# Phase tables of a state-space branch: from doubling on VectorE to sine and double angle on GpSimd and ScalarE

## The chip, the cores and the metric

The kernel runs on one core of a Trainium2 chip. The metric is the device time of one execution in microseconds (us), from the first to the last instruction and what lies around it. The engines are TensorE (PE in the rows, with its weight loads as PEld), VectorE (DVE), ScalarE (ACT), GpSimd (POOL) and SyncE (SP), which issues nearly all transfers. Each engine takes its instructions strictly in the order in which the program issued them.

## The reference, cut to what matters

One step of a decoder layer: 2048 prompt positions and 8 sample positions of width 1024. One input projection feeds a causal convolution branch (31 taps, layer norm, SiLU gate) and a state-space (SSM) branch; both are gated, merged, projected and normalised. The SSM branch, with 32 groups of 64 complex states:

```python
dt = exp(log_dt); mag = exp(a_re * dt)
lb = mag * (cos(a_im * dt) + i sin(a_im * dt))        # one step of a state
bb = ((lb - 1) / a) * b
s[t] = lb * s[t-1] + bb @ u[t];  y[t] = Re(c @ s[t]) + d * u[t]
```

The kernel computes the recurrence in blocks of 8 positions. A block multiplies a state by lb to the 8th power, that is by rho = mag to the 8th and a turn by 8 times the angle. The turn is taken out: the inputs of the block recurrence are turned back by k times that angle (k = 0 to 127), a real scan with factor rho runs, and its results are turned forward again. The cosines and sines of k times the angle, for 16 x 128 states and 128 values of k, are the phase tables.

## The kernel before, in words

The prompt is done in two halves of 1024 positions (`half`, from line 1078), the sample positions with the first. Weights come as 512 KB tiles by SP (`w_dma`), two buffers; ACT casts a tile's high part (`whi`, line 251) and POOL subtracts it for the low part (`wlo`, through `ew`, line 331). `stages` (lines 276 to 296) does three matmuls for each product, high by high, high by low and low by high (lines 288 to 290), into one of six PSUM banks, which ACT or DVE evicts. A first half's stage of one weight tile lasts some 11 us. The order of the stages is: embedding, `sx` (SSM inputs, eight short stages), then for eight column tiles the gate `sg` (a sigmoid on ACT) and `u` (a product on DVE), then further gates.

All other work is written as generators (tasks) that `Background` interleaves with the stages at the time the program is built. A task yields an engine and a ready time; `use` adds a fixed charge to that engine's clock (`cV`, `cS`, `cG` for DVE, ACT and POOL, such as 0.08 + n / 960 us); `pump` always takes the task that can start first by these clocks, up to the matmul clock. So the charges fix, in advance, where in each engine's order an instruction lies. On the chip only semaphores count: if an instruction comes later than charged, whatever is queued behind it on its engine, and on others that need it, waits.

The task `ssm_setup` (lines 448 to 658, priority 6) first computes dt, mag and the angle on DVE (32 and 7 small instructions; L180, L183 and L177 are the helpers `ts`, `stt` and `tt`, tile `spar`), a sine and half-angle sine on ACT (L481, L482), the powers of lb and the product `bb`; POOL copies the reversed powers and fills the block tables `cbd` (L522 to L537). It then makes the phase tables (tile `ph`) on DVE, in two halves of 8 state columns: three doublings bring the angle to 8 times its value, then seven doublings along k fill 128 values. Each doubling normalises a complex number and does a complex product of six instructions:

```python
while m < P:
    unit_length(un[0][:, :, m - 1], un[1][:, :, m - 1], s2)
    cmul(un[0][:, :, m:2 * m], un[1][:, :, m:2 * m], un[0][:, :, 0:m], un[1][:, :, 0:m], *base, ...)
    m *= 2
    r0 = use("V", 2.0 + 6 * cV(4 * m), r0)
```

Behind them, in four rounds, come the product tables: DVE computes `gt` from `pwr` and `bb` (six instructions of 128x512, tile `gw`), PE transposes it (L609) and multiplies it with `cbd` (L619), ACT and DVE copy the results (`we`, L612; `kd`), POOL computes `cq` (six instructions, L645), and SP writes everything to DRAM (`we_d`, `tt_d`, `cq_d`, `ph_d`).

`ssm_batch` (four per half) waits in the planner for its round's tables, reads `we` and the phases, multiplies on PE (L719), turns and scans on DVE, and ends in more matmuls (L774, L777). `conv_task` does the convolution taps on DVE into PSUM (`acc`, L183) and, if eight of the 38 shared buffers (`units`) are free, hands part of them to `conv_side`, which lets ACT scale (`cq`, L881) and POOL add (`ca`, L331). `rms_task` sums squares (`re`, `rt`, L984) for later norms. The embedding's and the first norm's splits (`hh`, `hl`) feed the `sx` stages.

Of the kernel before, what the change touches and what calls it, by code (L numbers as in the profile page):

```python
# [13 lines left out]
P = 128  # L14
# [119 lines left out]
def build(nc, tc, A, O):  # L134
# [23 lines left out]
    with ExitStack() as ctx:  # L158
# [53 lines left out]
        P_OF = {k: 8 // v for k, v in KT_OF.items()}  # L212
        BLOCKS = [[(0, 344), (344, 344), (688, 344)], [(0, 512), (512, 512)]]
        PARTS = [[[0], [1, 2]], [[0], [1]]]
        TOK = [HT + NS, HT]

        order = []
# [210 lines left out]
            tt(oim, t1, t2, ALU.add)  # L428

        MAGIC = 12582912.0  # L430

        def exp_dve(out, x, w, ki):

# [10 lines left out]
            ts(ki, k, 127.0, 8388608.0, ALU.add, ALU.mult)  # L444
            tt(out, q, ki.bitcast(F32))

        tables = {"done": 0}

        def ssm_setup():
            yield from room(4)  # L450
# [16 lines left out]
            exp_dve(dt, k3, (k1, k2), ki)  # L467
            tt(th, are, dt)
            exp_dve(mag, th, (k1, k2), ki)
            r0 = use("V", 5.6, 3.0)  # L470
            yield "V", r0
            tt(th, aim, dt)
            ts(k1, th, 0.15915494309189535, MAGIC)
# [2 lines left out]
            stt(th, k1, -1.9350051879882812e-3, th, ALU.mult, ALU.add)  # L476
            stt(th, k1, -3.0199157663446332e-7, th, ALU.mult, ALU.add)
            ts(th, th, -3.1415925, 3.1415925, ALU.max, ALU.min)
            r0 = use("V", 1.6, r0)
            yield "S", r0  # L480
            S.activation(out=sn, in_=th, func=AF.Sin)  # L481
            S.activation(out=k1, in_=th, func=AF.Sin, scale=0.5)  # L482
# [19 lines left out]
            tt(k2, nre, aim)  # L502
            tt(k1, k1, k2, ALU.subtract)
            tt(fim, k1, k3)
            r0 = use("V", 4.0, r0)
            yield "V", r0

            def powers(t, top):
# [13 lines left out]
                    GP.tensor_copy(out=pwrev[r][:, p, :], in_=pw[r][:, 7 - p, :])  # L522
            fb = [f.rearrange("p (j x) -> p j x", x=1).to_broadcast([P, NJ, 16]) for f in (fre, fim)]
            cmul(b3(bb, 0), b3(bb, 1), fb[0], fb[1], b3(bcu, 0), b3(bcu, 1), b3(bb, 2), b3(bb, 3))
            r0 = use("V", 6.0, r0)
            use("G", 1.5, r0)
            GP.memset(zero, 0.0)
            yield from room(2)
# [10 lines left out]
            yield None, r1  # L539
            for b in range(NB):  # L540
                dma(out=tt_d[b], in_=zero.rearrange("p (q x) -> p q x", q=1).to_broadcast([P, 8, P]))

            yield "V", r0
            tt(k1, mag, mag)
            tt(k1, k1, k1)
            tt(rho, k1, k1)
            ph = [[k1, k2], [k3, nre]]

            def unit_length(re, im, t):

                tt(t[0], re, re)
                tt(t[1], im, im)
                tt(t[0], t[0], t[1], ALU.add)
                ts(t[0], t[0], -0.5, 1.5)
                tt(re, re, t[0])
                tt(im, im, t[0])

            v2 = [wk[:, x * 16:x * 16 + 16] for x in range(2)]
            V.tensor_copy(out=ph[0][0], in_=cs)
            V.tensor_copy(out=ph[0][1], in_=sn)  # L560
            for x in range(3):
                unit_length(*ph[0], v2)
                cmul(*ph[1], *ph[0], *ph[0], *v2)
                ph.reverse()
            r0 = use("V", 6.5, r0)
            for x in range(2):
                yield from room(3)
                pu2 = [alloc(name="ph") for _ in range(3)]
                un = [t[:, 0:1024].rearrange("p (j k) -> p j k", k=P) for t in pu2[0:2]]
                w2 = [pu2[2][:, y * 512:(y + 1) * 512].rearrange("p (j k) -> p j k", j=8) for y in range(2)]  # L570
                s2 = [t[:, 0:8] for t in v2]
                yield "V", r0
                for r in range(2):
                    V.tensor_copy(out=un[r][:, :, 0], in_=ph[0][r][:, x * 8:x * 8 + 8])
                m = 1
                while m < P:
                    unit_length(un[0][:, :, m - 1], un[1][:, :, m - 1], s2)
                    base = [u_[:, :, m - 1:m].to_broadcast([P, 8, m]) for u_ in un]
                    cmul(un[0][:, :, m:2 * m], un[1][:, :, m:2 * m], un[0][:, :, 0:m], un[1][:, :, 0:m],
                         *base, w2[0][:, :, 0:m], w2[1][:, :, 0:m])  # L580
                    m *= 2
                    r0 = use("V", 2.0 + 6 * cV(4 * m), r0)
                    yield "V", r0
                for b in range(2 * x, 2 * x + 2):
                    for r in range(2):
                        dma(out=ph_d[b][:, r * 512:(r + 1) * 512],
                            in_=pu2[r][:, (b - 2 * x) * 512:(b - 2 * x + 1) * 512], after=r0)
                free(*pu2)
            r1 = max(r0, r1)
            for b in range(NB):  # L590
                js = slice(b * 4, b * 4 + 4)
                yield from room(6)
                gt = alloc(name="gt")
                wt = alloc(name="gw")
                v4 = lambda t, r: t[:, r * 512:(r + 1) * 512].rearrange("p (j d c) -> p j d c", d=8, c=16)
                pr = [pwrev[r][:, :, js].rearrange("p d (j c) -> p j d c", c=1).to_broadcast([P, 4, 8, 16])
                      for r in range(2)]
                br = [b3(bb, r)[:, js, :].rearrange("p j (d c) -> p j d c", d=1).to_broadcast([P, 4, 8, 16])
                      for r in range(2)]
                yield "V", r1  # L600
                cmul(v4(gt, 0), v4(gt, 1), pr[0], pr[1], br[0], br[1], v4(wt, 0), v4(wt, 1))
                r1 = use("V", 6 * cV(512), r1)
                we = alloc(name="we")
                wev = we[:, 0:1024].rearrange("p (j i r s) -> p j i r s", i=2, r=2, s=64)
                for r in range(2):
                    yield "P", r1
                    pt = bank()
                    for j in range(4):
                        T.transpose(pt[:, j * P:(j + 1) * P], gt[:, r * 512 + j * P:r * 512 + (j + 1) * P], ident)  # L609
                    r2 = use("P", 0.5, r1)  # L610
                    yield "S", r2
                    S.copy(out=wev[:, :, :, r, :], in_=pt.rearrange("p (j i s) -> p j i s", i=2, s=64))  # L612
                    r2 = use("S", cS(512), r2)
                yield "P", r1
                pt = bank()
                for j in range(4):
                    o = pt[:, j * 32:(j + 1) * 32]
                    for r in range(2):
                        T.matmul(o, gt[:, r * 512 + j * P:r * 512 + (j + 1) * P],  # L619
                                 cb[r][:, b * 4 + j].rearrange("p i c -> p (i c)"), start=r == 0, stop=r == 1)  # L620
                r3 = use("P", 1.0, r1)
                free(gt)
                yield "V", r3
                kdu = alloc(name="kd")
                kd, dd = [kdu[:, x * 128:(x + 1) * 128].rearrange("p (c g) -> p c g", g=8) for x in range(2)]
                q3 = slice(96, 128)
                tt(dd[q3], dtile[q3, b * 8:b * 8 + 8].rearrange("p (c g) -> p c g", c=1).to_broadcast([32, 16, 8]),
                   ident[q3, 112:128].rearrange("p (c g) -> p c g", g=1).to_broadcast([32, 16, 8]))
                V.tensor_copy(out=kd, in_=pt[:, 0:128].rearrange("p (g c) -> p c g", c=16))
                tt(kd[q3], kd[q3], dd[q3], ALU.add)  # L630
                r3 = use("V", 0.8, r3)
                yield None, max(r2, r3)
                dma(out=we_d[b], in_=we[:, 0:1024])
                for q in range(8):
                    dma(out=tt_d[b][0:(q + 1) * 16, q, :],
                                 in_=kdu[(7 - q) * 16:128, 0:128])
                free(kdu, we)
                cq = alloc(name="cq")
                pr = [pw[r][:, 1:9, js].rearrange("p d (j c) -> p j d c", c=1).to_broadcast([P, 4, 8, 16])
                      for r in range(2)]  # L640
                cr = [c3[r][:, js, :].rearrange("p j (d c) -> p j d c", d=1).to_broadcast([P, 4, 8, 16])
                      for r in range(2)]
                yield "G", r1
                t1, t2 = v4(wt, 0), v4(wt, 1)
                g = lambda o, x, y, op=ALU.mult: GP.tensor_tensor(out=o, in0=x, in1=y, op=op)  # L645
                g(t1, pr[0], cr[0])
                g(t2, pr[1], cr[1])
                g(v4(cq, 0), t1, t2, ALU.add)
                g(t1, pr[0], cr[1])
                g(t2, pr[1], cr[0])  # L650
                g(v4(cq, 1), t1, t2, ALU.subtract)
                r2 = use("G", 6 * cG(512), r1)
                yield None, r2 + 2.0
                dma(out=cq_d[b], in_=cq[:, 0:1024])
                free(cq, wt)
                tables["done"] = b + 1
                tables[b] = queue["data"] + 1.0
            free(bb, bcu, cbd, pu)


# [14 lines left out]
        def ssm_batch(h, b, sx, ysb, n, ready):  # L675
# [22 lines left out]
            yield from room(4)  # L698
            we = alloc(name="swe")
            r = max(r, dma(out=we[:, 0:1024], in_=we_d[b], after=tables[b]))  # L700
            phu = alloc(name="sph")
            rp = dma(out=phu[:, 0:1024], in_=ph_d[b], after=tables[b])
            sc = alloc(name="sc")
            X = sc[:, 0:1096].rearrange("p (r j s) -> p r j s", r=2, j=4)
            yield "V", 0.0
# [20 lines left out]
                        S.copy(out=smp[:, rr, b * 4 + j0:b * 4 + j0 + 2, :], in_=pvs[rr][:, :, 128:136])  # L726
                    r1 = use("S", 0.56 if first else 0.36, r1)
            free(we)
            r = max(r1, rp)
            tmp, tm2 = alloc(name="stmp"), alloc(name="stmq")  # L730
            E = X[:, :, :, 9:137]
            t1 = tmp[:, 0:1024].rearrange("p (r j s) -> p r j s", r=2, j=4)
# [853 lines left out]
```

## Time and profile before

| | |
|---|---|
| median of three runs | 1972.55 us (1971.04 to 1973.43) |
| the profiled execution's own time | 1971.99 us |
| its span, first to last instruction | 1970.2 us |
| mean granted clock of TensorE | 0.989 of full speed |
| PE busy | 1918.5 us, 97% of the span |
| DVE busy | 1442.1 us, 73% |
| ACT busy | 765.6 us, 39% |
| POOL busy | 784.8 us, 40% |

The rows give, for a group of instructions, their line, engine and operation, the tiles written and read, the shape and count, the busy time and the mean of one; in a timeline the start and length in us, and in brackets how long the engine sat idle before and which instruction ended that. A granted clock of 1.00 is 2.4 GHz and 0.50 is 1.2 GHz. Matmul records overlap, since matmuls are pipelined; the chain of waits gives the step from one to the next.

### The profile page before, as it was taken

Reading aid. Unit: us, or ns where it says so; the run is one execution under the profiler, and the core shown is the slowest. Engines: PE = TensorE matmul, PEld = TensorE weight load, DVE = VectorE, ACT = ScalarE, POOL = GpSimd, SP = SyncE. Lnnn points to the kernel's source line nnn. Section 1 sums busy time; section 2 is a strip of 40 time slices with the busy share of each in tenths; the row PEclk is TensorE's granted clock in tenths of the full one; section 3 lists DMA queues with packets and bytes.
Section 4 is the critical chain, followed back from the end, with each engine's and each line's share of the span. In section 5 each row is a group of like instructions: output and inputs, shape, how many; then the busy total and the mean of one; then the engine's idle time right before and its main releaser. Section 6 shows DMA issues by size and latency. Waiting matters only on the chain.

```text
span 1970.2 us, 26641 instructions
## 1 busy us (share of the span) xinstructions
PE 1918.5 (97%) x10386; PEld 1723.0 (87%) x10386; DVE 1442.1 (73%) x1696; ACT 765.6 (39%) x1276; POOL 784.8 (40%) x573
## 2 busy tenths in 40 slices
PE   8897999999999999999899999999999999999998
PEld 7797999999999999999798788888888888888877
DVE  6889997899899876444884479888589843442686
ACT  7424211227311364254532223444731353223542
POOL 1437623315422223253533222687743222224554
PEclk9998999999999999999899999999999999999999
DMA  8461344542122215342554463212212211422455
GB/s 315 155 203 62 100 133 141 177 144 78 51 83 78 102 50 193 116 142 93 190 197 164 172 200 123 74 60 91 71 48 75 97 67 43 160 107 77 148 189 174
DMA packets 103286, 243.58 MB, mean 124 GB/s; under 512 B 11752, under 2 KB 44648, under 8 KB 103144
## 3 DMA queue, kind: packets, MB, share of 16 engines
q1 hardware_dynamic: 102840, 241.68, 36.2%
q8 instruction: 81, 1.33, 0.3%
q14 instruction: 45, 0.37, 0.1%
q10 hardware_dynamic: 320, 0.20, 0.0%
HBM read 188.17 MB, written 54.62 MB: 123 GB/s over the span
## 4 chain that ended last, share of the span: by engine, by line
PE 85%; issue 4%; DVE 4%; POOL 2%; ACT 1%; DMA 1%; POOLq 0%; ACTq 0%; SPq 0%; DVEq 0%
PE bank L288 27%; PE bank L290 26%; PE bank L289 26%; PE bank L774 2%; POOL wlo L331 1%; PE bank L777 1%; PE bank L719 1%; DMA raw<-in_w 1%; POOL ca L331 1%; DVE sgp L331 1%; DVE o L183 0%; DVE o L331 0%; DVE ml L331 0%; DVE spar L183 0%; PE bank L308 0%
## 5 line engine op out<-in xcount | busy, mean ns | idle before, releaser
L331 POOL TENSOR_TENSOR wlo<-raw,whi 128x512 fp32r<-128x512 f32 x386 | 566.5, 1486 | 1082.2 <-ACT whi L251 1064.5
L288 PE MATMUL bank<-hh,whi 128*128 128x344 f32 (+1 forms) x1888 | 665.9, 353 | 0.9 <-ACT whi L251 0.9
L289 PE MATMUL bank<-hl,whi 128*128 128x344 f32 (+1 forms) x1888 | 659.9, 350 | 6.8 <-DVE hl L331 6.8
L290 PE MATMUL bank<-hh,wlo 128*128 128x344 f32 (+1 forms) x1888 | 661.2, 350 | 1.4 <-POOL wlo L331 1.4
L183 DVE SCALAR_TENSOR_TENSOR acc<-u,prm,acc 128x1024 f32<-128x1024 f32 x412 | 530.5, 1288 | 11.2
L289 PEld LDWEIGHTS bank<-hl,whi 128*128 128x128 f32 x1888 | 356.9, 189 | 39.4 <-DVE hl L331 7.1
L288 PEld LDWEIGHTS bank<-hh,whi 128*128 128x128 f32 x1888 | 356.4, 189 | 36.9 <-ACT whi L251 1.5
L290 PEld LDWEIGHTS bank<-hh,wlo 128*128 128x128 f32 x1888 | 356.8, 189 | 35.6 <-POOL wlo L331 2.4
L251 ACT CAST whi<-raw 128x512 fp32r<-128x512 f32 x388 | 223.9, 619 | 148.5 <-PE bank L289 68.6
L288 PE MATMUL bank<-mh,whi 128*128 128x344 f32 (+1 forms) x640 | 227.4, 355 | 7.7 <-ACT whi L251 5.8
L290 PE MATMUL bank<-mh,wlo 128*128 128x344 f32 (+1 forms) x640 | 227.1, 355 | 5.2 <-POOL wlo L331 5.1
L289 PE MATMUL bank<-ml,whi 128*128 128x344 f32 (+1 forms) x640 | 226.6, 354 | 0.3 <-DVE ml L331 0.3
L331 POOL TENSOR_TENSOR ca<-ca,cq 128x512 f32<-128x512 f32 x104 | 132.2, 1300 | 39.5 <-ACT cq L881 36.1
L288 PEld LDWEIGHTS bank<-mh,whi 128*128 128x128 f32 x640 | 122.6, 192 | 20.8 <-ACT whi L251 7.1
L290 PEld LDWEIGHTS bank<-mh,wlo 128*128 128x128 f32 x640 | 122.7, 192 | 18.9 <-POOL wlo L331 7.8
L289 PEld LDWEIGHTS bank<-ml,whi 128*128 128x128 f32 x640 | 122.5, 191 | 12.3 <-DVE ml L331 1.1
L289 PE MATMUL bank<-vl,whi 128*128 128x344 f32 (+1 forms) x320 | 111.9, 350 | 0.7 <-DVE vl L331 0.7
L288 PE MATMUL bank<-vh,whi 128*128 128x344 f32 (+1 forms) x320 | 112.2, 351 | 0.0
L290 PE MATMUL bank<-vh,wlo 128*128 128x344 f32 (+1 forms) x320 | 112.0, 350 | 0.0
L881 ACT ACTIVATE cq<-u,prm 128x512 f32<-128x512 f32 x104 | 73.4, 722 | 55.0 <-POOL ca L331 45.9
L331 DVE TENSOR_TENSOR oacc<-oacc,sq 128x344 f32<-128x344 f32 (+1 forms) x35 | 30.6, 874 | 79.2 <-ACT sq L1388 78.7
L177 DVE TENSOR_TENSOR gcl<-bank,gcl 128x344 f32<-128x344 f32 (+1 forms) x40 | 23.5, 587 | 65.7 <-PE bank L290 65.7
(213 smaller groups left out, 2447.7 us busy)
## 6 DMA issues: line engine op xcount, KB each, us to landing
raw<-in_w SPq DMA_DIRECT2D x194, 512.0 KB
cq<-cq SPq DMA_DIRECT2D x12, 512.0 KB
e<-e SPq DMA_DIRECT2D x8, 516.0 KB
rt<-e SPq DMA_DIRECT2D x8, 516.0 KB
gc<-gc SPq DMA_DIRECT2D x8, 516.0 KB
m<-gs SPq DMA_DIRECT2D x8, 516.0 KB
gcl<-gc SPq DMA_DIRECT2D x8, 516.0 KB
m2l<-m SPq DMA_DIRECT2D x8, 516.0 KB
```

The source lines that it names most:

```text
L177: V.tensor_tensor(out=out, in0=a, in1=b, op=op)
L183: V.scalar_tensor_tensor(out=out, in0=a, scalar=s, in1=b, op0=op0, op1=op1)
L251: S.copy(out=hi, in_=t[:, c])
L288: T.matmul(o, hi[:, w], rh[:, c0:c0 + n], start=kt == 0, stop=False)
L289: T.matmul(o, hi[:, w], rl[:, c0:c0 + n], start=False, stop=False)
L290: T.matmul(o, lo[:, w], rh[:, c0:c0 + n], start=False, stop=kt == k - 1)
L331: (V if e == "V" else GP).tensor_tensor(out=out, in0=a, in1=b, op=op)
L719: T.matmul(pvs[rr][half_[i], jj], we[:, g * P + rr * 64:g * P + rr * 64 + 64], U[:, g, 8:8 + ne], start=True, stop=True)
L774: T.matmul(pvs[i][:, jj], TW[:, :, 2 * j + i], U[:, 2 * j + i, o0:136], start=True, stop=False)
L777: T.matmul(pvs[i][:, jj], cq[half_[i], x * 512 + j * P:x * 512 + (j + 1) * P], X[half_[i], x, j, o0:136], start=False, stop=x == 1)
L881: S.activation(out=q[:, h], in_=u[:, k + x * 512:k + x * 512 + 512], func=AF.Identity, scale=w(k))
```

## The change

The doubling loops and `unit_length` go. The angle, brought to within half a turn, is turned into a part of a half turn and split into a coarse `hi` and a rest `lo`, with nine more small DVE instructions. A new task `phase_task` (priority 6.1) computes for each half of the columns the 1024 angles as k times `hi` and k times `lo` on POOL, takes away whole turns with two DVE instructions, and then uses sine and cosine of half the angle on ACT, their squares, and the double angle on POOL and DVE. `kk` holds the integers 0 to 127 plus one. The product tables follow the set-up directly, rho is computed earlier, several charges of the planner for the set-up are raised, and `ssm_batch` reads its phase table behind its first matmuls, after a wait of the planner for it. `OUT_PARTS` is not used.

```diff
-            r0 = use("V", 5.6, 3.0)
+            r0 = use("V", 11.0, 3.0)
...
-            r0 = use("V", 1.6, r0)
+
+            hi, lo, t1, t2 = [w(i) for i in range(11, 15)]
+            ts(t1, th, 12288.0, None, ALU.add)
...
+            stt(lo, th, 1.2732395447351628 - 1.2734375, lo, ALU.mult, ALU.add)
+            r0 = use("V", 2.5, r0)
...
-            r0 = use("V", 4.0, r0)
+            r0 = use("V", 7.0, r0)
+            yield "V", r0
+
+
+            tt(rho, mag, mag)
+            tt(rho, rho, rho)
+            tt(rho, rho, rho)
+            kk = pu[:, 944:1072]
+            yield "G", 0.0
+            GP.memset(kk[:, 0:1], 1.0)
+            m = 1
+            while m < P:
+                GP.tensor_scalar(out=kk[:, m:2 * m], in0=kk[:, 0:m], scalar1=float(m), scalar2=None, op0=ALU.add)
+                m *= 2
+            use("G", 3.5)
+
+            def phases(x, r):
+                yield from room(4)
+                pu2 = [alloc(name="ph") for _ in range(4)]
+                a, q, sp, cp = [t[:, 0:1024] for t in pu2]
...
+                yield "G", r
+                r = ew("G", v3(a), kb, part(hi), ALU.mult, 1024, r)
+                r2 = ew("G", v3(cp), kb, part(lo), ALU.mult, 1024, r)
+                yield "V", r
+                ts(q, a, MAGIC, None, ALU.add)
+                stt(a, q, -MAGIC, a, ALU.add, ALU.subtract)
+                r = max(use("V", cV2(1024) + cV(1024), r), r2)
+                yield "G", r
+                r = ew("G", a, cp, a, ALU.subtract, 1024, r)
+                yield "S", r
+                S.activation(out=q, in_=a, func=AF.Abs)
+                S.activation(out=sp, in_=a, func=AF.Sin, scale=PI)
+                S.activation(out=cp, in_=q, func=AF.Sin, scale=-PI, bias=hpi)
+                S.activation(out=a, in_=sp, func=AF.Square)
+                S.activation(out=q, in_=cp, func=AF.Square)
+                r = use("S", 5 * cS(1024) + 2.6, r)
+                yield "G", r
+                ew("G", sp, sp, cp, ALU.mult, 1024, r)
+                r = ew("G", cp, a, q, ALU.add, 1024, r)
+                yield "V", r
+                ts(cp, cp, -1.0, 2.0)
+                r2 = use("V", cV2(1024), r)
+                yield "G", r
+                r = ew("G", q, q, a, ALU.subtract, 1024, r)
+                yield "G", max(r, r2)
+                r = ew("G", q, q, cp, ALU.mult, 1024, max(r, r2))
+                yield "V", r2
+                stt(sp, sp, 2.0, cp, ALU.mult, ALU.mult)
...
+            bg.add(phase_task(r0), 6.1)
             yield "V", r0
...
-            r0 = use("V", 6.0, r0)
+            r0 = use("V", 8.0, r0)
...
-            for x in range(3):
-                unit_length(*ph[0], v2)
-                cmul(*ph[1], *ph[0], *ph[0], *v2)
-                ph.reverse()
-            r0 = use("V", 6.5, r0)
-            for x in range(2):
...
-                while m < P:
-                    unit_length(un[0][:, :, m - 1], un[1][:, :, m - 1], s2)
...
-                    r0 = use("V", 2.0 + 6 * cV(4 * m), r0)
-                    yield "V", r0
...
             free(we)
-            r = max(r1, rp)
+            while tables["phases"] < b + 1:
+                yield None, bg.now + 1.0
+            yield from room(3)
+            phu = alloc(name="sph")
+            r = max(r1, dma(out=phu[:, 0:1024], in_=ph_d[b], after=tables["ph", b // 2]))
```

## Rows read from the trace of the kernel before

**Rows 1.** Busy time on the page: us, share of the span, instructions.
```profile
PE 1918.5 (97%) x10386; PEld 1723.0 (87%) x10386; DVE 1442.1 (73%) x1696; ACT 765.6 (39%) x1276; POOL 784.8 (40%) x573
```
**Rows 2.** Busy time by stretches; after the engines: granted clock, DMA share, GB/s.
```profile
150.00:200.00 50.00, 35.92 (x219) 35.67 (x218) 48.86 (x71) 20.39 (x32) 35.39 (x28) 0.85 0.21 66
182.00:196.00 14.00, 0.09 (x1) 0.00 (x0) 13.58 (x24) 0.68 (x2) 4.55 (x4) 0.60 0.22 75
196.00:202.00 6.00, 5.83 (x22) 5.86 (x23) 5.90 (x10) 1.21 (x2) 1.28 (x1) 0.51 0.27 90
```
**Rows 3.** Waits of PE, whole span: us in total, times, longest.
```profile
PE bank L609 <- issue: 14.1, 1, 14.1
PE bank L288 <- ACT whi L251: 13.1, 6, 6.3
PE bank L289 <- DVE hl L331: 6.8, 1, 6.8
```
**Rows 4.** The chain that ended last, 196 to 204 us: start, length.
```profile
196.17 1.09 PE bank L609 x4
197.26 0.29 PE bank L288
...
202.23 0.15 PE bank L288
...
203.18 0.44 PE bank L609 x4
```
**Rows 5.** Timeline of DVE, 124 to 200 us.
```profile
124.59 0.62 DVE L177 TENSOR_TENSOR ph<-ph 128x64 f32<-128x64 f32 x3
...
157.44 3.78 DVE L177 TENSOR_TENSOR ph<-ph 128x64 f32<-128x64 f32 x3
...
192.17 0.69 DVE L177 TENSOR_TENSOR ph<-ph 128x512 f32<-128x512 f32 x1
...
197.43 0.69 DVE L177 TENSOR_TENSOR gt<-gw 128x512 f32<-128x512 f32 x1
```
**Rows 6.** Timeline of POOL at 152 us, in the second half of the phase tables.
```profile
152.31 7.58 POOL L331 TENSOR_TENSOR ca<-ca,cq 128x512 f32<-128x512 f32 x6 [0.62 <-ACT cq L881]
```
**Rows 7.** Busy time by stretches, over the phase tables on DVE.
```profile
105.20:192.80 87.60, 76.89 (x488) 76.61 (x486) 83.83 (x228) 32.58 (x54) 47.18 (x39) 0.95 0.39 122
```
**Rows 8.** Timeline of DVE around the set-up, and one wide tensor-scalar instruction.
```profile
69.21 0.16 DVE L180 TENSOR_SCALAR spar<-prm 128x16 f32<-128x16 f32 x1
...
83.17 0.87 DVE L331 TENSOR_TENSOR hl<-xT,hh 128x688 fp32r<-128x688 f32 x1
...
97.30 0.44 DVE L177 TENSOR_TENSOR bb<-bb 128x256 f32<-128x256 f32 x1
...
104.06 1.23 DVE L331 TENSOR_TENSOR re<-re,rt 128x1032 f32<-128x1032 f32 x1 [5.18 <-ACT rt L984]
...
451.96 0.70 DVE L180 TENSOR_SCALAR re<-re 128x1032 f32<-128x1032 f32 x1
```
**Rows 9.** Groups of POOL by line and shape: busy, mean ns, idle before.
```profile
L645 POOL TENSOR_TENSOR gw<-pw,bcu 128x512 f32<-128x512 f32 x16 | 17.7, 1127 | 0.3
L331 POOL TENSOR_TENSOR z<-z,zt 128x1024 f32<-128x1024 f32 x4 | 9.6, 2403 | 7.6 <-ACT zt L322 5.9 <-PE bank L290 1.7
```
**Rows 10.** Groups of ACT by line, in the same form.
```profile
L984 ACT ACTIVATE rt<-rt 128x1024 f32<-128x1024 f32 (+1 forms) x21 | 22.3, 1064 | 6.4 <-DMA rt<-e 6.4
L1154 ACT ACTIVATE z<-ysb 128x1024 f32<-128x1024 f32 x8 | 18.0, 2279 | 0.1
L322 ACT ACT_TABLE_LOAD x13 | 16.7, 1283 | 0.3
```
**Rows 11.** A late weight cast on ACT's timeline, and PE in its stretch.
```profile
337.90 0.62 ACT L251 CAST whi<-raw 128x512 fp32r<-128x512 f32 x1 [9.64 <-POOL cq L645]
...
300.00:350.00 50.00, 50.00 (x329) 48.93 (x329) 40.76 (x50) 8.29 (x17) 14.89 (x14) 1.00 0.48 145
```
**Rows 12.** Timeline of SP's queue: writes of the second half of the phase tables.
```profile
190.83 3.36 SPq L153 DMA_DIRECT2D ph<-ph  x4
```

More of the change, by code (lines that the diff above doesn't have):

```diff
@@ L214, in build @@
         PARTS = [[[0], [1, 2]], [[0], [1]]]
+        OUT_PARTS = [[[(0, 258), (258, 258)], [(516, 258), (774, 258)]], [[(0, 512)], [(512, 512)]]]
         TOK = [HT + NS, HT]
@@ L430, in build @@
         MAGIC = 12582912.0
+        PI = 3.141592653589793
+        hpi = sm([P, 1], "hpi")
+        V.memset(hpi, PI / 2)
         def exp_dve(out, x, w, ki):
@@ L445, in exp_dve @@
             tt(out, q, ki.bitcast(F32))
-        tables = {"done": 0}
+        tables = {"done": 0, "phases": 0}
         def ssm_setup():
@@ L478, in ssm_setup @@
             ts(th, th, -3.1415925, 3.1415925, ALU.max, ALU.min)
-            r0 = use("V", 1.6, r0)
+            hi, lo, t1, t2 = [w(i) for i in range(11, 15)]
+            ts(t1, th, 12288.0, None, ALU.add)
+            ts(t1, t1, -12288.0, None, ALU.add)
+            tt(t2, th, t1, ALU.subtract)
+            ts(t1, t1, 1.2734375)
+            ts(hi, t1, 1536.0, None, ALU.add)
+            ts(hi, hi, -1536.0, None, ALU.add)
+            tt(lo, t1, hi, ALU.subtract)
+            stt(lo, t2, 1.2734375, lo, ALU.mult, ALU.add)
+            stt(lo, th, 1.2732395447351628 - 1.2734375, lo, ALU.mult, ALU.add)
+            r0 = use("V", 2.5, r0)
             yield "S", r0
@@ new lines, in ssm_setup @@
+            use("G", 3.5)
[3 more added lines that the diff above has]
+                a, q, sp, cp = [t[:, 0:1024] for t in pu2]
+                v3 = lambda t: t.rearrange("p (j k) -> p j k", k=P)
+                kb = kk.rearrange("p (j k) -> p j k", j=1).to_broadcast([P, 8, P])
+                part = lambda t: t[:, x * 8:x * 8 + 8].rearrange("p (j k) -> p j k", k=1).to_broadcast([P, 8, P])
+                yield "G", r
[26 more added lines that the diff above has]
+                stt(sp, sp, 2.0, cp, ALU.mult, ALU.mult)
+                r = max(use("V", cV(1024), r2), r)
+                yield None, r
+                for b in range(2 * x, 2 * x + 2):
+                    c = slice((b - 2 * x) * 512, (b - 2 * x + 1) * 512)
+                    for k, t in enumerate((q, sp)):
+                        dma(out=ph_d[b][:, k * 512:(k + 1) * 512], in_=t[:, c], after=r)
+                free(*pu2)
+                tables["phases"] = 2 * x + 2
+                tables["ph", x] = queue["data"] + 1.0
@@ L506, in ssm_setup, with phase_task @@
+            def phase_task(r):
+                for x in range(2):
+                    yield from phases(x, r)
+            bg.add(phase_task(r0), 6.1)
             yield "V", r0
@@ L541, in ssm_setup @@
                 dma(out=tt_d[b], in_=zero.rearrange("p (q x) -> p q x", q=1).to_broadcast([P, 8, P]))
-            yield "V", r0
[L544 to L560, printed above, removed]
-            for x in range(3):
-                unit_length(*ph[0], v2)
-                cmul(*ph[1], *ph[0], *ph[0], *v2)
-                ph.reverse()
-            r0 = use("V", 6.5, r0)
-            for x in range(2):
[L567 to L575, printed above, removed]
-                while m < P:
-                    unit_length(un[0][:, :, m - 1], un[1][:, :, m - 1], s2)
[L578 to L581, printed above, removed]
-                    r0 = use("V", 2.0 + 6 * cV(4 * m), r0)
[L583 to L588, printed above, removed]
             r1 = max(r0, r1)
@@ L657, in ssm_setup @@
                 tables[b] = queue["data"] + 1.0
+            while tables["phases"] < NB:
+                yield None, bg.now + 0.5
             free(bb, bcu, cbd, pu)
@@ L700, in ssm_batch @@
             r = max(r, dma(out=we[:, 0:1024], in_=we_d[b], after=tables[b]))
-            phu = alloc(name="sph")
-            rp = dma(out=phu[:, 0:1024], in_=ph_d[b], after=tables[b])
             sc = alloc(name="sc")
```

## The prediction, made before the changed kernel was run

> **What bounds the kernel now.** I read first the busy shares, then the busy time by stretches, then the waits of the matmul engine, then the chain around the one large hole, and last what each other engine did there. TensorE (PE) is busy 97% of the span [rows 1], so a change to other engines counts only where PE waits. One stretch stands out: in 150 to 200 us PE is busy 35.92 of 50 us, and in 182 to 196 us it does next to nothing, while VectorE (DVE) is busy 13.58 of those 14 us [rows 2]. The list of PE's waits gives the same hole a name: 14.1 us ahead of line 609, the transposes of the product table `gt`; all its other waits are shorter, and of late DVE products only one costs over 1 us, 6.8 us near 77 us, ahead of the stretch in question [rows 3]. The label says "issue" because the wait stands in PE's own queue. The chain shows the price behind the hole: the first transposes take 1.09 us where the next group takes 0.44, and the matmuls behind them run at 0.29 us where they later run at 0.15 [rows 4], at a granted clock of 0.51, the 1.2 GHz level [rows 2]. Sixteen matmuls at 0.13 to 0.14 us extra are 2.1 us, the transposes 0.65: 2.7 us. Hole and slow restart together cost 14.1 + 2.7 = 16.8 us.
>
> Why is `gt` late? DVE takes its orders in sequence, and between 105 and 193 us they are the phase tables. The last phase product starts at 192.17 and the last `gt` product, five instructions of that table later, at 197.43 [rows 5]. The order was fixed by a planner which charges one half of the phase tables 7 x 2.0 us + 6 x (7 x 0.08 + 4 x 127 / 960) = 20.5 us. The second half lasted from 141.9 to 192.8, 50.9 us, about 6 of them other work. The rows say why: three products of 128x64 take 0.62 us while GpSimd (POOL) is idle and 3.78 us while POOL adds convolution taps at 1.26 us each [rows 5, 6]. So the planner put the transposes into PE's queue long before their data.
>
> **Removed.** 210 DVE instructions (17 normalisations of 6, 17 complex products of 6, 6 copies) disappear; in their stretch DVE was busy 83.83 us [rows 7], of which some 8.5 were evictions, sums and the first convolution instructions, so about 75 us. On PE's path lies only what they delay: the 16.8 us. The rest of the freed DVE time goes to the convolution, for which PE does not wait.
>
> **Moved.** The product tables no longer stand behind the phase tables. By the planner's charges `gt` followed the start of the set-up after 5.6 + 1.6 + 1.9 + 4.0 + 6.0 + 6.0 + 6.5 + 41 = 72.6 us; with the raised ones it follows after 11.0 + 2.5 + 1.9 + 7.0 + 8.0 + 6.0 = 36.4. So the transposes enter PE's queue some 36 us before 182, near 145 us. The last of `bb`, which `gt` reads, was ready at 97.7 us [rows 8]. With the additions below I put the first `gt` at 112 to 125 us. The price of a new wait ahead of line 609: 0 us if it is that early, up to 11 us by the row of slowed products (six at about 1.3 to 2.4 us next to POOL, less the planner's own 5 us for them). I take 1 us, since the charges now lie near what the trace shows. All four transposes, their copies and POOL's products move forward alike; they cost the same as before, only elsewhere.
>
> The set-up's first batch (32 instructions from 69.21 to 83.26 us) does not change, and the split of the activations queued behind it, for which PE waits 6.8 us [rows 3, 8], still stands there. Value 0; bounds: a gain of 5 us if the higher charge sent that split to POOL, no loss.
>
> **Added on DVE.** Nine instructions for the split of the angle, at 0.17 us alone and up to 1.3 beside POOL: 1.6 to 12 us, on a DVE that idles 5.18 us ahead of 104 us [rows 8] and is rid of 75. Each phase table adds two tensor-scalar instructions of about 0.70 us [rows 8] and two with a second tensor of about 1.3, twice the product of 512 columns at 0.69 [rows 5]: 4 us, 8 for both. Cost to PE 0; without that cover they would delay `gt` again.
>
> **Added on POOL.** Eight tiny instructions for the row of integers, and per table seven of 128x1024. Two read broadcasts (nearest row 1.127 us for 512, so 2.25), five are plain (2.40) [rows 9]: 16.5 us per table, 33 for both. In 150 to 200 us POOL is busy 35.39 of 50 [rows 2], in 105 to 193 it is 47.18 of 87.6 [rows 7], so there is room for 33 us, but not for the moved table products (six of 1.1 to 1.3 us, 7 us, four times) as well without pressure. What is queued behind them on POOL are the low parts of the weights.
>
> **Added on ScalarE (ACT).** Five passes per table. Sine is only seen on 16 columns, so its width is priced by the squares of 1024 columns, 1.064 us [rows 10]; bounds 1.06 and 2.28 (the Gelu pass of that width). Since the sigmoids of the gate run there, a table load before and one after, 1.283 us each [rows 10]: 5.3 + 2.6 = 7.9 us per table. Behind it in ACT's queue lie evictions and the high parts of the weights. What covers it: at 337.9 us a weight cast came 9.64 us late behind POOL's products, and PE was busy 50.00 of 50 us [rows 11]. So one lump of 7.9 us fits. Bounds for both lumps and POOL together: 0 (each alone, as in that row) to 6 us (a lump that meets POOL's products). I take 1.5. The Trainium skill (ScalarE: Activation LUTs, What ACT_TABLE_LOAD costs) adds a drain and puts a switch at about 2.66 us; by that the lump would be 10.6 us and the estimate about 1 us higher, which no row here shows.
>
> **Queues.** SP issues the same eight writes of the phase tables, four at a time (3.36 us) [rows 12], now behind the new chain; a late table would hold the weight loads behind it. Value 0, since four such writes stood at 190.83 too and the load after them was not waited for. The read of a phase table moves behind the state matmuls and its wait for the table is one of the planner, with no instruction queued behind it on an engine; the state chain starts earlier than before, so nobody waits.
>
> **Sum.** The profiled execution took 1971.99 us, 0.56 below the median of 1972.55. 1971.99 - 16.8 + 1.0 + 1.5 = 1957.7; against the median 1958.3.
>
> **Rivals.** (a) The wait returns at line 609. POOL's passes of 2.4 us slow the two-tensor DVE instructions of the set-up as the 1.26 us ones slowed the phases [rows 5, 6]. For: the slowed rows. Against: only 16.5 us of POOL stand ahead of the first `gt`, in three pieces. Price: up to 11 us of the 14.1 remain, with half the slow clock; mean case about +8 on the forecast, 1966. The Trainium skill (SBUF — State Buffer, Who interferes with whom) says this as a rule: POOL and a DVE instruction with two SBUF inputs exclude each other for a whole instruction. By that rule the moved work would hand DVE waits twice as long, which is this rival; the slowed trio agrees that there are such waits.
>
> (b) Slower: ACT's lump waits for POOL. The five passes stand in ACT's queue for POOL's difference; if that lies W us behind the plan, the weight casts behind come 7.9 + W late. With the 9.6 us of cover from above, PE loses W - 1.7 us per table. It decides at W = 10 (gain eaten in two tables); W = 12 gives 2 x 10.3 - 16.8 = +3.8: 1976. That needs the products of a table (7 us) and a weight split (2.6 us) ahead of the difference, both times. For: POOL's pressure. Against: the planner charges POOL 2.30 for what takes 2.40.
>
> (c) No effect: the product tables are still held by units, since the phase tables now take four buffers of 38 beside the six that `gt` asks for; PE's hole moves and keeps its size: 1972.
>
> **How the numbers follow.** Forecast 66%, (a) 16%, (b) 11%, (c) 7%. The forecast's own range is 1953 (the 5 us bound of the split) to 1963; with (a) it reaches 1968, which leaves out (b), (c) and the tail of (a), a fifth. A measurement here can tell about 0.2%, 3.9 us, from no change: faster is below 1968.6, so the forecast and three quarters of (a), 78%; same is (c) and the rest of (a), 11%; slower (b), 11%.
>
> **What would show it.** Right: line 609 gone from PE's waits, transposes before 155 us, the clock at 1.00 through 180 to 205 us, DVE free of phase products, and on ACT two lumps of about 8 us with two table loads each. Wrong: a wait of more than 4 us at line 609 (rival a); PE waits for the weight casts between 100 and 200 us, with ACT idle ahead of the absolute value (rival b); a hole of 10 us elsewhere before 250 us (rival c).

## The result, and the profile after

The changed kernel takes 1988.8 us (median of four runs, 1988.08 to 1991.74) against 1972.99 us for the kernel before on the same chip: a ratio of 1.0084, 95% interval 1.0066 to 1.0101. It is 0.8% slower; the forecast was 1958.0. The profiled execution took 1989.09 us, with a span of 1987.0 us. New lines are numbered 1 to 37 higher up: the transposes of `gt` are L642 (were L609), the scans L787 (L750), the last state matmuls L811 and L814 (L774, L777).

The page's busy times, answering to [rows 1]:

```profile
PE 1924.8 (97%) x10386; PEld 1727.0 (87%) x10386; DVE 1387.2 (70%) x1481; ACT 818.9 (41%) x1343; POOL 900.0 (45%) x641
```

PE was busy 6.3 us longer with the same number of matmuls, so it ran longer at the lower clock (mean granted clock 0.984 against 0.989), and it was idle 10.5 us longer: the span grew by 16.8 us. Its waits, answering to [rows 3]:

```profile
PE bank L289 <- ACT whi L252: 14.3, 6, 6.9
PE bank L814 <- DVE sc L177: 11.0, 4, 4.6
PE bank L814 <- DMA cq<-cq: 11.0, 1, 11.0
...
PE bank L290 <- DVE hl L332: 5.3, 1, 5.3
```

The 14.1 us at the transposes are gone: L642 is not in the list. In their place stand five waits at L814, 22.0 us in all. Busy time by stretches, the first two answering to [rows 2]:

```profile
150.00:200.00 50.00, 49.74 (x340) 49.01 (x340) 49.14 (x50) 17.38 (x31) 40.39 (x24) 1.00 0.41 132
182.00:196.00 14.00, 14.00 (x91) 14.00 (x90) 13.72 (x14) 8.09 (x15) 12.22 (x9) 1.00 0.42 126
...
200.00:250.00 50.00, 46.23 (x298) 43.50 (x296) 48.57 (x66) 8.76 (x25) 11.99 (x9) 0.93 0.38 126
300.00:350.00 50.00, 38.99 (x263) 36.89 (x262) 48.50 (x48) 20.99 (x44) 37.81 (x26) 0.86 0.25 85
```

Before 200 us the hole went, as forecast. The holes are now at 225 us (3.8 us), at 343 us (11.0) and in 1200 to 1300 us (7.3 in three). The chain of waits through the largest one:

```profile
331.90 1.18 DVE acc L183
333.08 2.18 DVE stmp L177
335.26 2.21 DVE stmq L177
...
337.50 2.25 DVE sc L177 x2
...
339.76 3.51 DMA cq<-cq
...
343.41 1.28 PE bank L814 x8
```

The profile calls this a wait for a transfer, but the transfer was only issued when DVE finished the last turn of a state chain, at 339.75 us. DVE's timeline shows why that was late:

```profile
316.13 2.31 DVE L177 TENSOR_TENSOR stmq<-sc,sph 128x1024 f32<-128x1024 f32 x1
318.48 3.37 DVE L177 TENSOR_TENSOR sc<-stmp,stmq 128x512 f32<-128x512 f32 x2
...
322.19 9.70 DVE L787 TENSOR_TENSOR_SCAN sc<-rho,sfin,sc 128x128 f32<-128x128 f32 x8
331.82 1.26 DVE L183 SCALAR_TENSOR_TENSOR acc<-u,prm,acc 128x1024 f32<-128x1024 f32 x1
...
340.99 1.22 DVE L177 TENSOR_TENSOR stmq<-sc,sph 128x1024 f32<-128x1024 f32 x1
342.24 1.29 DVE L177 TENSOR_TENSOR sc<-stmp,stmq 128x512 f32<-128x512 f32 x2
```

And POOL's at the same time:

```profile
304.77 8.97 POOL L332 TENSOR_TENSOR ca<-ca,cq 128x512 f32<-128x512 f32 x7
...
317.31 12.55 POOL L332 TENSOR_TENSOR ca<-ca,cq 128x512 f32<-128x512 f32 x8
...
332.92 5.66 POOL L332 TENSOR_TENSOR ca<-ca,cq 128x512 f32<-128x512 f32 x3
```

While POOL adds convolution taps, eight scans take 9.70 us, a product of 1024 columns 2.31 and two of 512 take 3.37; a few us later, without adds, the products take 1.22 and 1.29. The `acc` instruction between them, whose `acc` is in PSUM, keeps its 1.26 us. These are the side path's adds, the same that slowed the doubling in [rows 5, 6]. Before, the side path opened at 150 us, beside the doubling, and then not before 1228 us; now it opens at 298 us, beside the later state chains of the first half, at 425 us, behind them, and from 1157 us beside those of the second (150 adds in all, against 104). All 64 scans took 41.4 us, against 25.8. Ahead of the hole at 225 us products take 2.31 us too, but POOL's work there is the low parts of the weights, not adds:

```profile
218.28 2.31 DVE L177 TENSOR_TENSOR stmq<-sc,sph 128x1024 f32<-128x1024 f32 x1
```

```profile
217.88 1.63 POOL L332 TENSOR_TENSOR wlo<-raw,whi 128x512 fp32r<-128x512 f32 x1 [0.60 <-ACT whi L252]
```

### The profile page after: what moved, and what is told of

Read it like the earlier page. It is cut to its first block, busy times and chain, and to the rows that moved or that the text cites. A ratio compares the mean times of both kernels' runs of the same rounds, so it can differ in the third digit from the quotient of the medians.

```text
span 1987.0 us, 26568 instructions
## 1 busy us (share of the span) xinstructions
PE 1924.8 (97%) x10386; PEld 1727.0 (87%) x10386; DVE 1387.2 (70%) x1481; ACT 818.9 (41%) x1343; POOL 900.0 (45%) x641
## 4 chain that ended last, share of the span: by engine, by line
PE 77%; DVE 12%; issue 4%; ACT 2%; POOL 1%; DMA 1%; SPq 0%; DVEq 0%; POOLq 0%; ACTq 0%
PE bank L289 24%; PE bank L291 24%; PE bank L290 24%; DVE acc L183 2%; PE bank L811 1%; DVE sc L787 1%; POOL wlo L332 1%; PE bank L814 1%; DVE sc L177 1%; DVE stmq L177 1%; DVE stmp L177 1%; DMA raw<-in_w 1%; DVE o L332 1%; DVE o L183 1%; DVE sgp L332 1%
## 5 line engine op out<-in xcount | busy, mean ns | idle before, releaser
L332 POOL TENSOR_TENSOR wlo<-raw,whi 128x512 fp32r<-128x512 f32 x386 | 574.5, 1507 | 957.5 <-ACT whi L252 929.4
L183 DVE SCALAR_TENSOR_TENSOR acc<-u,prm,acc 128x1024 f32<-128x1024 f32 x389 | 500.8, 1287 | 10.5
L332 POOL TENSOR_TENSOR ca<-ca,cq 128x512 f32<-128x512 f32 x150 | 205.9, 1403 | 61.6 <-ACT cq L918 59.1
L289 PEld LDWEIGHTS bank<-mh,whi 128*128 128x128 f32 x640 | 122.3, 191 | 23.2 <-ACT whi L252 7.8
L918 ACT ACTIVATE cq<-u,prm 128x512 f32<-128x512 f32 x150 | 106.4, 724 | 83.0 <-POOL ca L332 79.5
L332 DVE TENSOR_TENSOR cz<-cz,u 128x1032 f32<-128x1032 f32 (+1 forms) x16 | 21.8, 1364 | 83.2 <-ACT cz L323 83.2
```

Source lines behind the costliest of these rows:

```text
L183: V.scalar_tensor_tensor(out=out, in0=a, scalar=s, in1=b, op0=op0, op1=op1)
L289: T.matmul(o, hi[:, w], rh[:, c0:c0 + n], start=kt == 0, stop=False)
L332: (V if e == "V" else GP).tensor_tensor(out=out, in0=a, in1=b, op=op)
L918: S.activation(out=q[:, h], in_=u[:, k + x * 512:k + x * 512 + 512], func=AF.Identity, scale=w(k))
```

## The experiments

The theory after the first look: **the hole was moved, not removed.** Both holes have one cause. DVE's work slows beside the side path's adds, the planner's charges don't know it, so PE's matmuls stand in its queue ahead of their data. The rivals: the charges of the set-up were simply too low (the prediction's reason), or DVE's own doubling is what counts.

**Side path held in the changed kernel** until all state chains of the half have been issued.

```diff
-                if units.left() >= 8:
+                if units.left() >= 8 and all(t[3] for t in tables["ssm"]):
```

> The changed kernel with one condition more: the convolution's side path (ACT scales, POOL adds) is only opened for a channel when the planner has issued all SSM chains of that half. Theory T (the side path's adds on POOL slow the turns and scans of the SSM chains on DVE, and PE waits for those at line 814): the waits of 11.0 and 7.3 us at line 814 go, the scans at 322 and 1226 us take 3.1 us in place of 9.7 and 10.1, one wait of some 4 us near 225 us may stay; about 1965 to 1970 us. Rival P (the phase work on POOL and ACT itself makes DVE late): the waits stay or move, over 1980 us. Rival L (the planner places the SSM matmuls too early whatever runs beside): waits at line 814 of 10 us or more in all, over 1978 us.

Measured: 1965.6 us, 0.9964 of before (0.9950 to 0.9978), 23.2 us below the changed kernel and as theory T had it. PE's wait at L814:

```profile
PE bank L814 <- DMA cq<-cq: 4.0, 1, 4.0
```

The stretch of the largest hole, by windows, and a group of scans on DVE's timeline:

```profile
300.00:400.00 100.00, 100.00 (x664) 96.73 (x664) 90.39 (x99) 24.85 (x56) 21.30 (x15) 1.00 0.40 139
```

```profile
319.50 3.10 DVE L787 TENSOR_TENSOR_SCAN sc<-rho,sfin,sc 128x128 f32<-128x128 f32 x8
```

Of 22.0 us, 4.0 stay, those near 225 us, where no side path was open in the changed kernel either.

**The same in the kernel before**, with a wait for a free buffer ahead of `kd`.

> The kernel before with the same condition on the side path (and one planner's wait for a free buffer ahead of the table copies). The doubling stays on DVE. Theory T (the hole of 14.1 us at line 609 came from the side path running beside the doubling): the three products of 128x64 take about 0.6 us in both halves of the table, the hole shrinks to 4 us or less, 1956 to 1963 us. Rival D (the doubling's own length on DVE makes the hole): 10 us or more of it stay, 1968 to 1975 us.

Measured: 1979.2 us, 1.0035 (1.0022 to 1.0048). The end of the first table's `gt` on DVE's timeline, the stretch of the old hole by windows, and PE's longest wait:

```profile
180.30 0.69 DVE L177 TENSOR_TENSOR gt<-gw 128x512 f32<-128x512 f32 x1
```

```profile
100.00:200.00 100.00, 100.00 (x643) 99.96 (x642) 89.68 (x261) 33.09 (x56) 41.01 (x39) 1.00 0.46 147
```

```profile
PE bank L288 <- ACT vh L338: 14.7, 3, 6.0
```

Without adds that `gt` comes at 180.30 instead of 197.43 us [rows 5], 17.1 us earlier, and the hole is gone, with charges unchanged. The expected time is missed all the same: DVE has to double and do all of the first half's convolution itself, its end comes late, and PE waits for `vh` between 400 and 800 us (busy 381.5 of 400).

**The adds without their reading.** In the changed kernel each add of the side path becomes two zero fills on POOL; charges, order and places stay. This leaves out the side path's share of the convolution.

```diff
-  left["r"] = free_at[x] = ew("G", a2[:, h], a2[:, h], q[:, h], ALU.add, 512, r)
+  GP.memset(a2[:, h], 0.0)
+  GP.memset(a2[:, h], 0.0)
+  left["r"] = free_at[x] = use("G", cG(512), r)
```

> The changed kernel with each side-path add on POOL replaced by two fills of the same half row with zero, charged as the add was, so that the planner issues all else in the same order; the side path's share of the convolution is left out. Theory T (POOL's reads and DVE's two-tensor instructions exclude each other): scans back at 3.1 us, the waits of 11.0 and 7.3 us at line 814 at 2 us or less, 1965 to 1971 us. Rival L (order alone): waits as in the changed kernel, 1983 us or more.

Measured: 1963.9 us, 0.9954 (0.9939 to 0.9969). A group of scans on DVE's timeline, and POOL's at the same time:

```profile
319.04 3.10 DVE L787 TENSOR_TENSOR_SCAN sc<-rho,sfin,sc 128x128 f32<-128x128 f32 x8
```

```profile
318.08 0.52 POOL L921 MEMSET ca<- 128x512 f32 x1
318.66 0.53 POOL L922 MEMSET ca<- 128x512 f32 x1
```

POOL has fills to do in that stretch without a gap, but it only writes, and the scans are back at 3.10 us; 4.0 us stay at L814. A fill (0.53 us) is shorter than an add (1.3), but the scans lost nothing at all. What slows DVE is not a busy POOL but POOL's reading. The Trainium skill (SBUF — State Buffer, Who interferes with whom) says that a DVE instruction with two SBUF inputs contends with a GpSimd instruction that reads SBUF, "not with one that only writes it". These traces agree, `acc` from PSUM included.

**The raised charges alone** in the kernel before (11.0, 2.5, 7.0, 8.0 for 5.6, 1.6, 4.0, 6.0).

> The kernel before with the four raised charges of the set-up alone (5.6 to 11.0, 1.6 to 2.5, 4.0 to 7.0, 6.0 to 8.0); the doubling stays on DVE ahead of the product tables. The prediction's step (the hole at line 609 is a matter of charges that are too low): the hole falls to 6 us or less, 1957 to 1966 us. Theory T: the result hangs on whether a channel's side path still runs beside the doubling; if POOL adds taps during the tables, 8 us or more of waits stay; if it does not, they are under 4 us.

Measured: 1981.6 us, 1.0042 (1.0027 to 1.0057); the hole keeps its size:

```profile
PE bank L609 <- DVE gt L177: 14.2, 1, 14.2
```

Doubling and side path moved together: POOL's first add starts at 155.06 us (152.31 before), so it still adds beside the doubling. Low charges of the set-up were not the cause of the hole.

**The changed kernel with charges that know the side path**: turns charged 2.25 times and scans 3.5 times as long while one is open; again a wait for a free buffer ahead of `kd`.

> The changed kernel with the side path as it is, but the planner charges the turns 2.25 times and the scans 3.5 times as much while a side path is open (and waits for a free buffer ahead of the table copies). Theory T (PE waits because the SSM matmuls' place was fixed by charges that know nothing of POOL): scans stay slow (over 6 us) where a side path is open, yet the waits at line 814 fall to 5 us or less in all; 1963 to 1973 us. Rival B (DVE simply has too much to do there): as much waiting turns up at other lines; over 1978 us.

Measured: 1961.5 us, 0.9939 (0.9924 to 0.9954). The scans (now L789) are as slow as ever, by DVE's timeline; four groups of eight take 9.70 to 11.09 us, where two took over 9 in the changed kernel. But PE's only wait at the state matmuls (now L816) is the early one:

```profile
323.98 9.70 DVE L789 TENSOR_TENSOR_SCAN sc<-rho,sfin,sc 128x128 f32<-128x128 f32 x8
```

```profile
PE bank L816 <- DMA cq<-cq: 3.9, 1, 3.9
```

That shows the second half of the theory: the slow scans cost PE nothing here, matmuls placed too early do. The time is even below the expected range. The added wait for a free buffer doesn't explain it: it also stands in the dose run below, which took as long as the changed kernel.

**Doubling in the changed order.** Changed order and charges, side path held, a wait for a free buffer ahead of `kd`, but the phase tables doubled on DVE as a task behind the product tables.

> The order and charges of the changed kernel, with the side path held back, but the phase tables still doubled on DVE, as a task behind the product tables. Theory S (the sine tables are worth what they take off DVE, about 50 us where nothing slows it): no wait over 3 us at line 609, but the convolution of the first half ends late and PE waits 10 us or more for the normed products near 780 us; 1972 to 1982 us. Rival O (only the order and the side path matter): 1963 to 1968 us, as with the sine tables.

Measured: 1989.6 us, 1.0085 (1.0068 to 1.0102), 24 us above the version with sine tables. PE's waits, and its stretch from 400 to 800 us by windows:

```profile
PE bank L289 <- ACT vh L339: 8.0, 5, 2.6
...
PE bank L290 <- DVE vl L332: 5.6, 5, 1.7
PE bank L625 <- DVE gt L177: 4.1, 4, 1.4
```

```profile
400.00:800.00 400.00, 384.86 (x2386) 379.46 (x2385) 332.36 (x329) 162.00 (x246) 133.82 (x92) 0.97 0.25 85
```

With sine tables PE is busy 398.9 of those 400 us. So DVE's time in the first half is worth something once the side path doesn't help, and more than expected (1972 to 1982 us). But 6.9 us of waits stand before 200 us, for `gt` and `kd`: part of the 24 us is again a matter of places.

**The early read.** The version with the side path held, and the read of `cq` issued only when the chain is ready in the plan.

> The changed kernel with the side path held back as in the run of that name, and the planner told that the read of cq ahead of line 814 starts only when DVE has turned the states back (its buffer is free only then). Theory: the 4.0 us that PE still waited there near 225 us, with the slow restart behind it, go; scans stay at 3.1 us; 1957 to 1963 us. Rival (that wait is DVE's own lag, which a later read does not cure): a wait of 3 us or more stays at line 814; 1964 to 1967 us.

Measured: 1962.6 us, 0.9942 (0.9926 to 0.9959), not separable from 1965.6. The time lies in the theory's range, but the mechanism is the rival's: the wait near 225 us became one of 3.7 us for DVE's turn itself. So the first chain is late on DVE, and the transfer only shares its buffer.

**The first chain placed later.** The version with honest charges, and this:

```diff
-  r = use("V", slow(3.5) * 8 * cV(256), r)
+  r = use("V", slow(3.5) * 8 * cV(256) + (4.5 if first and b == 0 else 0.0), r)
```

> The version with honest charges (1961.45 us) with 4.5 us more charged to the scans of the first state chain of the first half, nothing else. Theory of places (a matmul stands where the charges put it): the last wait at the state matmuls (now line 816), 3.9 us near 225 us, goes or falls below 1 us, the matmuls of the stages move up into its place, and the time is 1956.5 to 1958.5. Rival: VectorE's own lag only shows elsewhere, or the later release of the chain's buffers moves the side paths again; then a wait of 3 us or more stands somewhere else before 450 us and the time is 1961 or more.

Measured: 1956.0 us, 0.9899 (0.9884 to 0.9915), faster than both kernels and 0.5 us below the expected range. Its stretches by windows, and scans of both halves on DVE's timeline:

```profile
200.00:250.00 50.00, 49.61 (x336) 46.97 (x334) 48.88 (x64) 9.11 (x25) 12.66 (x10) 1.00 0.42 142
300.00:350.00 50.00, 50.00 (x358) 47.94 (x358) 46.94 (x61) 11.81 (x33) 13.55 (x11) 1.00 0.43 157
```

```profile
327.45 3.10 DVE L789 TENSOR_TENSOR_SCAN sc<-rho,sfin,sc 128x128 f32<-128x128 f32 x8
...
1207.45 10.08 DVE L789 TENSOR_TENSOR_SCAN sc<-rho,sfin,sc 128x128 f32<-128x128 f32 x8
```

At L816 PE waits 0.4 us in all. In the first half the side path moved to 378 us by itself, so its scans are quick again, and the 5.4 us against the version with honest charges can't be split between that and the place of the first chain; in the second half the scans are slow and nobody waits.

**Doubling with better places.** Two tries to mend the kernel before by charges alone: each doubling charged twice as long, with the turns and scans as above and waits for free buffers; and 10 us charged between phase and product tables.

> The kernel before, with doubling on VectorE, but with charges as they are beside a side path: the charge of each doubling twice as large, turns times 2.25 and scans times 3.5 while a side path is open, and two waits for free buffers. Theory of places alone (the sine tables are worth nothing by themselves, the hole was only a wrong place): the wait at line 609 falls from 14 to below 3 us, no other comes, 1955 to 1961 us. Rival, that VectorE's time is short in the first half when it doubles (as with the side path held there): the hole at line 609 goes, but waits for vh and vl on ScalarE and VectorE of 10 us or more in all appear between 400 and 950 us, and the time is 1967 to 1982; the sine tables are then worth 6 to 20 us against this version.

> The kernel before with one line more: 10 us charged to VectorE between the phase tables and the first product table, so that the planner puts the transposes of line 609 (now 610) some 11 us later into the matmul order; doubling, sine-free, and the side path in the first half stay as they were, six adds for six. Theory of places: the wait at line 610 falls from 14 us to 3 to 5, the slow restart behind it goes, and the time is 1960 to 1965 us; the sine tables, in the version with honest charges and a later first chain (1956.0), are then worth some 4 to 9 us beyond what a better place gives. Rival: the 10 us of charge push the state chains and the convolution back as the doubled charges did (2028 us), waits for vh, vl or tw appear after 400 us, and the time is 1968 or more.

Measured: 2028.4 us, 1.0265 (1.0248 to 1.0282), and 1993.9 us, 1.0094 (1.0072 to 1.0115). The longest waits of the first and the second:

```profile
PE bank L288 <- ACT vh L338: 23.0, 3, 14.3
PE bank L363 <- ACT nh L338: 21.0, 1, 21.0
...
PE bank L777 <- DMA tw<-tt: 13.3, 1, 13.3
```

```profile
PE bank L610 <- DVE gt L177: 12.5, 1, 12.5
...
PE bank L778 <- DVE sc L177: 8.0, 1, 8.0
```

The first missed both ranges; the second missed its theory and lies in its rival's range, with waits for `vh`, `vl` and `tw` after 400 us (8.5 us). In the first no hole is left before 400 us (PE busy 100.00 of each 100 us from 100 on), but tables, chains and convolution stand so late that the first half ends late. In the second the adds went on to 200 us (six of 8.89 us at 185.68), DVE's last products slowed too, and the first `gt` came at 205.70 instead of 195.38: the hole moved along. So what the sine tables are worth at good places on both sides stays open; shown are only the 24 us above, without side path, which hold some waits of place.

**A dose** (side path in the first half's second channel at five free buffers instead of eight) left the adds where they were: 1988.8 us, ratio 1.0078 (1.0063 to 1.0093), which says nothing on the dose.

> The changed kernel with the side path opened for the second channel of the first half at five free buffers in place of eight, so that it runs beside the first two SSM chains in place of the third. Theory T: the slow scans move with it: those at 213 and 226 us take over 5 us, waits at line 814 near 225 to 245 us grow from 3.8 to 8 us or more, and the wait of 11.0 us near 343 us goes; 1980 to 1995 us. Rival P (the wait belongs to the third chain, whatever runs beside it): it stays near 343 us.

## Why the prediction was wrong

**What held.** The hole with its slow restart went, as the sum had it: the first `gt` at 107.06 us (put at 112 to 125, so somewhat earlier still), transposes at 134.5 (before 155), no wait there, clock 1.00. POOL took 16.9 us for the first phase table (16.5). ACT's lumps are these, the first one:

```profile
139.88 1.06 ACT L553 ACTIVATE ph<-ph 128x1024 f32<-128x1024 f32 x1
140.96 1.28 ACT L554 ACT_TABLE_LOAD   x1
142.26 1.06 ACT L554 ACTIVATE ph<-ph 128x1024 f32<-128x1024 f32 x1
143.22 1.13 ACT L555 ACTIVATE ph<-ph,hpi 128x1024 f32<-128x1024 f32 x1
...
146.27 1.28 ACT L323 ACT_TABLE_LOAD   x1
147.56 0.46 ACT L323 ACTIVATE sg<-bank 128x344 f32<-128x344 f32 x1
```

7.68 us (7.9), sine at the price of the squares, the lower bound, and no PE wait behind it. By the Trainium skill (ScalarE: Activation LUTs, What ACT_TABLE_LOAD costs) there would be a drain as well; the first sine starts 1.30 us after its load does, and the load itself lasts 1.28, so none shows. ACT did stand 3.09 us behind POOL in the second lump, far from the 10 us from which rival (b) decides. The split `hl` gained nothing, as forecast: it starts at 84.00 us, against 83.17 before [rows 8].

```profile
84.00 0.87 DVE L332 TENSOR_TENSOR hl<-xT,hh 128x688 fp32r<-128x688 f32 x1
```

PE's wait for it is 1.5 us shorter only because PE came there later; the dose run, with the same set-up, waits 6.7 us.

**What failed** is the step under Queues: "the state chain starts earlier than before, so nobody waits". That step followed the planner's places for the chain but not DVE's time for it. The chain starts in a stretch where other work lies: the low parts of the weights on POOL near 225 us (3.8 us; that they make all of it is not shown), the side path near 343 us (11.0 us) and in the second half (7.3 us). Its price was taken as 0 and was 22.0 us in five waits, with slow clock behind them (0.86 in 300 to 350 us). Beside it fell "the rest of the freed DVE time goes to the convolution, for which PE does not wait": in the first half the convolution also decides when and where the side path opens. That it opened later because buffers came free at other times fits the rule of eight free buffers, but was only argued.

**The reason was half right.** The prediction read from [rows 5, 6] that adds slow DVE's two-tensor work, and used it for the set-up only, as rival (a). It then saw the raised charges as the safeguard; alone they changed nothing. Rival (c), the hole that moves and keeps its size, came nearest in kind, but by units of `gt` and before 250 us; the hole went to the other customer of the same contention and grew.

**The balance.** 14.1 us less at the transposes and 1.5 at `hl` (chance, as above), 22.0 more at L814, 3.5 at the smaller waits of ACT's and POOL's casts (`whi` +1.2, `mh` +1.7, `wlo` +0.6): +9.9 of the 10.5 us of idle time. With the side path held, the changed kernel is 7.3 us faster than the kernel before; with honest places 18.2 us (1974.2 to 1956.0), some 4 more than the sum had. Both set a mended changed kernel against the kernel before as it was, so neither is the worth of the sine tables alone.

## What to carry to other kernels

Where a fixed plan sets the order, removing work moves everything behind it: list what will lie beside each moved chain on the engine that shares its reads, before the waits there are priced at zero. A hole caused by contention is not cured by taking away its victim. What helped here was to move the other party, or, in the changed kernel, to charge the victim what it takes beside it. Higher charges are no safe side either: the kernel before became 54 us slower with them, though several were raised there at once.

## What the runs showed of the hardware

Scans of 128x128 suffer beside POOL's adds as products do: eight took 3.10 us alone or beside POOL's fills, and 9.70 to 11.09 beside its adds, 0.8 to 1.0 us more for each scan. A product of 1024 columns rose from 1.22 to 2.31 us, by 1.1, and two of 512 from 1.29 to 3.37, by 1.0 each. So the price of one instruction was much the same whatever its length, somewhat less than an add of 1.3 us, and short instructions paid most for their size. POOL paid too: eight adds beside the scans took 12.55 us, 1.57 each, against 1.28 in the seven from 304.77 us.
